# Down-projection weight sums taken by DRAM transfers during gate and up, paced by that stage

## The chip, the cores and the metric

One core of a Trainium2 chip runs the whole program. The metric is device time in microseconds (us), the median of several executions; lower is better. PE is TensorE (matrix products), DVE is VectorE, ACT is ScalarE, POOL is GpSimd and SP is SyncE, which here only issues DMA transfers. The kernel is written with a scheduling layer that decides the order on every engine when the program is built and adds all semaphore waits; on the chip every engine runs its list strictly in order.

## The reference, cut to what matters

The reference is one step of a two-layer backbone. In every layer a token mixer is followed by this channel mixer, on 640 tokens (512 + 128) of width 1024, with 2816 hidden units:

```python
def swiglu(h, w_gate_up, w_down):
    g, u = jnp.split(h @ w_gate_up, 2, axis=-1)
    return (jax.nn.silu(g) * u) @ w_down

    h2 = rmsnorm(x, g_pre_ffn) * (1.0 + scale2) + shift2
    x = x + gate2 * rmsnorm(swiglu(h2, w_gate_up, w_down), g_post_ffn)
```

All data are float32. The kernel splits each factor into a high and a low part (`split`, lines 211 and 217: ACT writes the rounded high part, DVE the difference) and takes three products per block (`mm3`, lines 227 to 229).

## The kernel before, in words

**Gate and up** (`gate_up`) makes the hidden activations in 22 steps of 128 units, j = 0 to 21; j = 0 and 1 are plain, the other twenty (`fast`) use seven products in place of eight (Strassen's scheme). Each step loads two blocks of 512 KB of weights by SP (line 969; I call them the first and the second load of a step) into `raw`, a pool of three buffers. `prep` makes four sums of quarters of these blocks on DVE (line 214, tile `sw`) and splits seven operands into `w` tiles, one step ahead of PE. The first sum (`sw<-raw,raw`) needs both loads. PE adds several products into one PSUM bank that ACT and DVE read in between, so PE waits if those reads are late; the last such read is DVE's `s<-ps,s` ahead of the seventh product. The result is `hid` (line 951). In layer 0 a list of background steps (`self.bg`) stands beside it: 8 loads of 1 MB and 32 DVE steps (tile `acc`) for the modulation of layer 1, one for each 6.6 us of the program's own count of time (`clk`).

**The down projection** (`w_down`) is Strassen's scheme over the whole stage: the hidden units are split in two (e), the output columns in two (h), and seven phases run one after another, in this order: p1, p2, p5, p6, p3, p7, p4. Each goes over six groups of hidden units, g = 0 to 5, a group holding 512 KB of weights per (e, h), the last one 256 KB. Phases p1, p2, p3 and p7 take 99 matrix instructions, p5, p6 and p4 take 66. Per group the phase splits the weights into `w` (`wsplit`) and the activations into `hs` (`xsplit`). p1, p2 and p3 use the blocks as they are. The other phases use sums of them:

- p5 uses W(0,0) + W(0,1), p6 adds W(1,1) to that, p4 adds W(1,0) as well. The running sum lies in SBUF in three `wk` tiles (`V`, filled by p1's load, line 1076); after each split POOL adds the next block by a DMA that accumulates (`add`, line 1079).
- p7 uses W(0,1) + W(1,1): SP loads the first into `raw` (`fresh`, line 1083), POOL adds the second by an accumulating DMA into the same buffer, and then ACT and DVE split it (line 1239).

So the POOL queue carries 24 accumulating DMAs per layer in the down projection. The normalisations (`rsq`, lines 248 to 252) are on the same queue. From p7 on, `begin` (line 1156), `finish` and `end` bring in the residual of finished tokens by SP, finish them on ACT, POOL and DVE (line 917) and store them by SP (line 1170); in layer 0 they are also prepared for the next layer. The `hs` tiles and these `work` tiles come from one pool of 12 buffers (`Q`).

Of the kernel before, what the change touches and what calls it, by code (L numbers as in the profile page):

```python
# [10 lines left out]
F32 = mybir.dt.float32  # L11
R = mybir.dt.float32r
AF = mybir.ActivationFunctionType
ALU = mybir.AluOpType
# [117 lines left out]
class Trunk:  # L132
# [811 lines left out]
    def gate_up(self, l, pre):  # L944
        nc, a, blk = self.nc, self.a, self.blk
        hid = [self.Q([4, N], F32, "hid") for i in range(NJ // 4)]

# [38 lines left out]
        def fast(j, ops, nxt):  # L986
# [13 lines left out]
            u, v = self.S(), self.S()  # L1000
# [20 lines left out]
            product(C, a12, blk[1][0], True, g11)  # L1021
            product(A, a22, t4, False, lambda: out(j, 0, A, g0, nc.vector))

        ws = [[self.load(a["w_gu"][l, j, u]) for u in range(2)] for j in range(NPLAIN)]
# [9 lines left out]
        for j in range(NPLAIN):  # L1034
            plain(j, ws[j], 1)
            for _ in range(8):
                next(nxt, None)
# [6 lines left out]

    def w_down(self, l, src, hid, gg, nxt):

# [11 lines left out]
        dd = [self.Q([3, 2, 384], F32, "dd") for _ in range(2)]  # L1058
        V = [None] * 3

# [8 lines left out]

        def vg(g):  # L1070
            return V[g // 2][:, (g % 2) * 1024 : (g % 2) * 1024 + cnt(g) * 512]

        def into(g, e, h):
            if V[g // 2] is None:
                V[g // 2] = self.W()
            nc.sync.dma_start(out=vg(g), in_=dram(e, h, g))

        def add(dst, e, h, g):
            nc.gpsimd.dma_start(out=dst, in_=dram(e, h, g), accum_op=ALU.add)

        def fresh(g, e, h):
            r = self.raw()[:, 0 : cnt(g) * 512]
            nc.sync.dma_start(out=r, in_=dram(e, h, g))
            return r

        def wsplit(g, s):
# [89 lines left out]
        def p1(g):  # L1176
            into(g, 0, 0)
            w = wsplit(g, vg(g))
            add(vg(g), 0, 1, g)
# [9 lines left out]
        def p2(g):  # L1189
            w = wsplit(g, fresh(g, 1, 0))  # L1190
            return xsplit(g, [x(g, 1)[:, :, A4]]), w
# [13 lines left out]
        def p5(g):  # L1205
            w = wsplit(g, vg(g))
            add(vg(g), 1, 1, g)
            return xsplit(g, [d(g)[:, :, 128:384]]), w
# [5 lines left out]
        def p6(g):  # L1214
            w = wsplit(g, vg(g))
            add(vg(g), 1, 0, g)
            s = d(g)[:, :, 128:384]
# [8 lines left out]
        def p3(g):  # L1226
            w = wsplit(g, fresh(g, 1, 1))
            s = d(g)[:, :, 128:384]
# [8 lines left out]
        def p7(g):  # L1237
            r = fresh(g, 0, 1)
            add(r, 1, 1, g)
            w = wsplit(g, r)  # L1240
            h = self.Q([2, 2, 384], R, "hs")
# [7 lines left out]
        def p4(g):  # L1249
            return xsplit(g, [x(g, 1)[:, :, B4]]), wsplit(g, vg(g))  # L1250

# [90 lines left out]
    def run(self):  # L1342
# [4 lines left out]
        for l in range(L):  # L1347
# [20 lines left out]
            pre = self.w_down(l, x, hid, gg, nxt)  # L1368
            if l + 1 < L:
# [41 lines left out]
```

## Time and profile before

| | us |
|---|---|
| median of 3 runs (lowest, highest) | 1390.4 (1387.85, 1395.24) |
| time of the profiled execution | 1396.39 |
| span of its trace, first to last instruction | 1394.5 |
| gate and up from j = 2 to the end, layer 0 | 318.4 to 568.4 |
| down projection, layer 0 | 568.4 to 716.6 |
| gate and up from j = 2 to the end, layer 1 | 996.1 to 1242.9 |
| down projection, layer 1 | 1242.9 to 1387.2 |
| tail after the last matrix instruction | 1387.2 to 1394.5 |

Read it as a line with two places of interest in each layer: the stage of gate and up, some 250 us, and the down projection behind it, some 145 us. The borders are the starts of the first matrix instruction of each stage. A matrix instruction is shown as busy for longer than the distance to the next one, because they are pipelined; so phases with the same number of instructions are compared by their length and not by their busy time.

### The profile page before, as it was taken

Reading aid. Unit: us, or ns where it says so; the run is one execution under the profiler, and the core shown is the slowest. Engines: PE = TensorE matmul, PEld = TensorE weight load, DVE = VectorE, ACT = ScalarE, POOL = GpSimd, SP = SyncE. Lnnn points to the kernel's source line nnn. Section 1 sums busy time; section 2 is a strip of 40 time slices with the busy share of each in tenths; the row PEclk is TensorE's granted clock in tenths of the full one; section 3 lists DMA queues with packets and bytes.
Section 4 is the critical chain, followed back from the end, with each engine's and each line's share of the span. In section 5 each row is a group of like instructions: output and inputs, shape, how many; then the busy total and the mean of one; then the engine's idle time right before and its main releaser. Section 6 shows DMA issues by size and latency. Waiting matters only on the chain.

```text
span 1394.5 us, 21421 instructions
## 1 busy us (share of the span) xinstructions
PE 1342.1 (96%) x8188; PEld 1206.2 (86%) x8188; DVE 1023.3 (73%) x1794; ACT 692.0 (50%) x1398; POOL 151.3 (11%) x186
## 2 busy tenths in 40 slices
PE   5899999999999999999899999999999999999996
PEld 2788977899999999888688998878999999998875
DVE  3789476499988985776788956757977777675955
ACT  4543275465554554545583324746644544444633
POOL 1101121110000000111211101302000000010220
PEclk9999999999999999999999999999999999999998
DMA  9555247244333333768655533553222322375982
GB/s 373 168 166 184 82 147 241 99 146 143 125 108 106 120 121 110 194 139 192 183 181 184 186 112 121 176 204 124 73 92 91 90 78 85 98 184 126 183 211 97
DMA packets 57974, 203.68 MB, mean 146 GB/s; under 512 B 7488, under 2 KB 8384, under 8 KB 56848
## 3 DMA queue, kind: packets, MB, share of 16 engines
q1 hardware_dynamic: 50960, 179.25, 38.7%
q0 software_dynamic: 6912, 23.07, 9.4%
q8 instruction: 64, 1.05, 0.3%
q14 instruction: 38, 0.31, 0.1%
HBM read 191.61 MB, written 10.68 MB: 145 GB/s over the span
## 4 chain that ended last, share of the span: by engine, by line
PE 71%; DMA 9%; DVE 8%; issue 5%; ACT 4%; POOL 2%; POOLq 0%; DVEq 0%; SPq 0%; ACTq 0%
PE ps L227 22%; PE ps L229 22%; PE ps L228 22%; DMA raw<-in_w_dn 4%; PE ps L240 2%; DVE w L217 2%; DVE acc L377 2%; PE ps L284 2%; ACT w L211 2%; DMA raw<-in_w_out 1%; PE ps L829 1%; POOL rt L252 1%; DMA raw<-in_ada 1%; DMA raw<-in_w_vpc 1%; DMA raw<-in_w_b 1%
## 5 line engine op out<-in xcount | busy, mean ns | idle before, releaser
L217 DVE TENSOR_TENSOR w<-raw,w 128x512 fp32r<-128x512 f32 (+2 forms) x220 | 197.5, 903 | 105.5 <-ACT w L211 104.0
L211 ACT ACTIVATE w<-raw 128x512 fp32r<-128x512 f32 (+2 forms) x220 | 175.4, 801 | 185.5 <-PE ps L229 74.8
L227 PE MATMUL ps<-T,w 128*128 128x320 f32 x640 | 198.5, 310 | 0.0
L229 PE MATMUL ps<-T,w 128*128 128x320 f32 x640 | 197.8, 309 | 0.0
L228 PE MATMUL ps<-T,w 128*128 128x320 f32 x640 | 197.7, 309 | 0.0
L227 PE MATMUL ps<-b,w 128*128 128x320 f32 x608 | 188.1, 309 | 0.0
L228 PE MATMUL ps<-b,w 128*128 128x320 f32 x608 | 187.9, 309 | 0.0
L229 PE MATMUL ps<-b,w 128*128 128x320 f32 x608 | 187.9, 309 | 0.0
L227 PE MATMUL ps<-w,hs 128*128 128x512 f32 x396 | 156.7, 396 | 6.6 <-ACT cc L211 4.6
L229 PE MATMUL ps<-w,hs 128*128 128x512 f32 x396 | 156.4, 395 | 5.5 <-DVE hs L217 5.4
L228 PE MATMUL ps<-w,hs 128*128 128x512 f32 x396 | 156.3, 395 | 0.2 <-DVE w L217 0.2
L211 ACT ACTIVATE w<-sw 128x512 fp32r<-128x512 f32 x160 | 96.3, 625 | 77.3 <-PE ps L229 65.3
L211 ACT ACTIVATE s<-ps 128x320 f32<-128x320 f32 (+2 forms) x148 | 65.3, 443 | 129.1 <-PE ps L229 105.9
L214 DVE TENSOR_TENSOR s<-ps,s 128x320 f32<-128x320 f32 (+1 forms) x144 | 68.7, 482 | 80.1 <-PE ps L229 79.9
L227 PEld LDWEIGHTS ps<-T,w 128*128 128x128 f32 x640 | 120.1, 188 | 2.1 <-issue 1.7
L228 PEld LDWEIGHTS ps<-T,w 128*128 128x128 f32 x640 | 120.1, 188 | 0.0
L229 PEld LDWEIGHTS ps<-T,w 128*128 128x128 f32 x640 | 120.1, 188 | 0.0
L227 PEld LDWEIGHTS ps<-b,w 128*128 128x128 f32 x608 | 114.1, 188 | 0.4 <-ACT s L211 0.3
L228 PEld LDWEIGHTS ps<-b,w 128*128 128x128 f32 x608 | 114.1, 188 | 0.1
L229 PEld LDWEIGHTS ps<-b,w 128*128 128x128 f32 x608 | 114.1, 188 | 0.0
L217 DVE TENSOR_TENSOR w<-sw,w 128x512 fp32r<-128x512 f32 x160 | 106.2, 686 | 5.1 <-ACT w L211 3.1
L227 PEld LDWEIGHTS ps<-w,hs 128*128 128x128 f32 x396 | 75.6, 191 | 23.8 <-ACT cc L211 5.4
(236 smaller groups left out, 2856.3 us busy)
## 6 DMA issues: line engine op xcount, KB each, us to landing
raw<-in_w_gu SPq DMA_DIRECT2D x88, 512.0 KB, 3.5
raw<-in_ada SPq DMA_DIRECT2D x64, 512.0 KB, 4.3
raw<-in_w_dn SPq DMA_DIRECT2D x30, 512.0 KB, 4.3
wk<-in_w_dn POOLq DMA_DIRECT2D x30, 512.0 KB, 6.2
ada<-in_ada SPq DMA_DIRECT2D x8, 1024.0 KB, 15.5
raw<-in_w_out SPq DMA_DIRECT2D x16, 512.0 KB, 4.1
wk<-in_ada SPq DMA_DIRECT2D x8, 1024.0 KB
xs<-work SPq DMA_DIRECT2D x15, 512.0 KB, 4.6
```

Source lines behind the costliest of these rows:

```text
L211: self.nc.scalar.activation(out, in_, f, **kw)
L214: self.nc.vector.tensor_tensor(out, x, y, op=op)
L217: self.nc.vector.tensor_tensor(lo, src, hi.bitcast(F32), op=ALU.subtract)
L227: mm(out, lh, rh, start=start, stop=False, skip_group_check=more)
L228: mm(out, lh, rl, start=False, stop=False, skip_group_check=more)
L229: mm(out, ll, rh, start=False, stop=stop, skip_group_check=more)
L240: self.nc.tensor.transpose(out, in_, self.ident)
L252: self.nc.gpsimd.tensor_tensor(r2, r, self.mhalf[:, :n], op=ALU.pow)
L284: self.nc.tensor.matmul(ps[32 * j : 32 * j + 32, :], self.cond[:, k, :], s, start=start, stop=stop, tile_position=(0, 32 * j))
L377: nc.vector.scalar_tensor_tensor(acc[:, s], raw, c, acc[:, s], op0=ALU.mult, op1=ALU.add)
L829: self.nc.tensor.matmul(ps[64 * e : 64 * e + 64, :], lhs[e], rhs[e], start=start, stop=stop, tile_position=(0, 64 * e))
```

## The change

The sums are made in DRAM during gate and up instead of in SBUF during the down projection. A new function `queue_sums` makes a list of 36 steps for POOL. They fill four scratch arrays in DRAM, v0 to v3, each with six groups: v0 = W(0,0) + W(0,1), v2 = W(0,1) + W(1,1), v1 = v0 + W(1,1), v3 = v1 + W(1,0). A sum is a copy from DRAM to DRAM and an accumulating DMA with its target in DRAM; the first 12 steps hold two DMAs each (v0 and v2), the other 24 one each, which makes 48 per layer. Each step begins with a copy of one element of `hid` by POOL, so that its transfers wait until gate and up has written that element. The steps go into the background list, in layer 0 alternating with those that were there; the distance of the list becomes 215 us divided by its length, and it starts later. In the down projection every phase now loads by SP into `raw` and splits from there: p5 from v0, p6 from v1, p7 from v2, p4 from v3.

```diff
+            self.pace = hid[j // 4][:, j % 4, 0:1]      # end of fast(j); plain(j) sets it too
...
+    def queue_sums(self, l):
+        v = [[self.dp.tile([128, 1040], F32, ...)[:, 0 : (2 if g < 5 else 1) * 512] for g in range(6)] for i in range(4)]
+        def copy(i, g, s):
+            nc.gpsimd.dma_start(out=v[i][g], in_=s)
+        def add(i, e, h, g):
+            nc.gpsimd.dma_start(out=v[i][g], in_=dram(e, h, g), accum_op=ALU.add)
+        def paced(f):
+            def go():
+                t = self.M([1], "pace", 2)
+                ins = nc.gpsimd.tensor_copy(t, self.pace)
+                with self.tc.issue_after(ins.ins):
+                    f()
+            return go
...
         def p7(g):
-            r = fresh(g, 0, 1)
-            add(r, 1, 1, g)
-            w = wsplit(g, r)
+            w = wsplit(g, vs[2][g])
...
         def p4(g):
-            return xsplit(g, [x(g, 1)[:, :, B4]]), wsplit(g, vg(g))
+            return xsplit(g, [x(g, 1)[:, :, B4]]), wsplit(g, vs[3][g])
...
+            vs, qs = self.queue_sums(l)
             if l + 1 < L:
                 mod1, q = self.queue_ada_w(l + 1, 0)
-                self.bg, self.bg_last = [(6.6, f) for f in q], self.now + 12.0
+                qs = [x for k in range(max(len(q), len(qs))) for x in (*q[k : k + 1], *qs[k : k + 1])]
+            self.bg, self.bg_last = [(215.0 / len(qs), f) for f in qs], self.now + 30.0
```

How the lists of the engines change, in layer 1. First POOL around gate and up, before the change: behind the last normalisation (`rs`, `rt`) of the stage ahead there stand at once the accumulating DMAs of the down projection into `wk`.

```order
L250 TENSOR_SCALAR rs_9536<-ms_9534 128x1
L252 TENSOR_TENSOR rt_9538<-rs_9536,mhalf 128x1
L1079 DMA wk_12374<-in_w_dn 128x1024 x2
L1079 DMA wk_12411<-in_w_dn 128x1024 x2
L1079 DMA wk_12466<-in_w_dn 128x1024
L1079 DMA wk_12466<-in_w_dt 128x512
```

The same place after it (`v` is a scratch array in DRAM, `pace` the copied element):

```order
L250 TENSOR_SCALAR rs_9719<-ms_9717 128x1
L252 TENSOR_TENSOR rt_9721<-rs_9719,mhalf 128x1
L1067 COPY pace_10135<-hid_9687 128x1
L1058 DMA v_9663<-in_w_dn 128x1024
L1058 DMA v_9675<-in_w_dn 128x1024
L1067 COPY pace_10211<-hid_9687 128x1
L1058 DMA v_9664<-in_w_dn 128x1024
L1058 DMA v_9676<-in_w_dn 128x1024
```

The waits on `hid` and the transfers now stand between the two stages' normalisations, where POOL had nothing in this stage. Next POOL at p7 of layer 1 before the change, with the additions into `raw` ahead of the normalisation of the first finished tokens:

```order
L1079 DMA raw_13115<-in_w_dn 128x1024
L1079 DMA raw_13151<-in_w_dn 128x1024
L1079 DMA raw_13187<-in_w_dn 128x1024
L248 TENSOR_SCALAR rs_13218<-mso_12363 128x1
L252 TENSOR_TENSOR rt_13220<-rs_13218,mhalf 128x1
L1079 DMA raw_13232<-in_w_dt 128x512
L248 TENSOR_SCALAR rs_13225<-mso_12364 128x1
```

After it, the last paced sums are directly followed by those normalisations:

```order
L1067 COPY pace_12567<-wk_12425 128x1
L1061 DMA v_9685<-in_w_dn 128x1024
L1067 COPY pace_12620<-wk_12425 128x1
L1061 DMA v_9686<-in_w_dt 128x512
L248 TENSOR_SCALAR rs_13525<-mso_12666 128x1
L252 TENSOR_TENSOR rt_13527<-rs_13525,mhalf 128x1
L248 TENSOR_SCALAR rs_13532<-mso_12667 128x1
```

The additions have left this place. Last, SP from the end of p7's loads on, layer 1, before the change (`work<-xs` is the load of a residual, `out_y_s<-work` the store of finished tokens):

```order
L1083 DMA raw_13187<-in_w_dn 128x1024
L278 DMA work_13146<-xs_9019 128x1024
L1083 DMA raw_13232<-in_w_dt 128x512
L278 DMA work_13182<-xs_9019 128x1024
L1170 DMA out_y_s<-work_13146 128x1024
L1170 DMA out_y_s<-work_13182 128x1024
```

After it, where v_9679 and v_9680 belong to p7 and v_9681 to v_9686 to p4:

```order
L1110 DMA raw_13495<-v_9679 128x1024
L1110 DMA raw_13539<-v_9680 128x512
L1110 DMA raw_13554<-v_9681 128x1024
L1110 DMA raw_13591<-v_9682 128x1024
L278 DMA work_13455<-xs_9178 128x1024
L1110 DMA raw_13611<-v_9683 128x1024
L1194 DMA out_y_s<-work_13455 128x1024
L278 DMA work_13490<-xs_9178 128x1024
L1110 DMA raw_13642<-v_9684 128x1024
L1110 DMA raw_13667<-v_9685 128x1024
L1194 DMA out_y_s<-work_13490 128x1024
L1110 DMA raw_13692<-v_9686 128x512
```

The six loads of p4, which were not there before, now stand among the loads and stores of the finished tokens. In layer 1 the lists of PE, ACT and DVE are otherwise the same up to the last step of gate and up; in layer 0 the background steps stand at other places in DVE's list.

## Rows read from the trace of the kernel before

**Rows 1.** The page: busy time of PE, its share of the span, and instructions.

```profile
PE 1342.1 (96%) x8188; PEld 1206.2 (86%) x8188; DVE 1023.3 (73%) x1794; ACT 692.0 (50%) x1398; POOL 151.3 (11%) x186
```

**Rows 2.** Busy time by stretch. Each row: from and to, length, then busy us and instructions of PE, PEld, DVE, ACT and POOL, the granted TensorE clock, the DMA share and GB/s. In order: gate and up of layer 0 and of layer 1; layer 0's p5 with p6, p3, p7, p4; layer 1's p3, p7, p4.

```profile
318.40:568.40 250.00, 250.00 (x1705) 247.50 (x1705) 215.99 (x357) 125.72 (x244) 2.83 (x3) 1.00 0.39 122
996.10:1242.90 246.80, 246.75 (x1683) 246.47 (x1682) 179.85 (x316) 122.30 (x239) 1.82 (x2) 1.00 0.32 99
...
613.30:643.20 29.90, 29.90 (x133) 24.76 (x132) 27.51 (x38) 19.57 (x31) 8.77 (x10) 1.00 0.99 181
643.20:665.70 22.50, 22.50 (x101) 18.60 (x101) 12.60 (x17) 11.16 (x17) 2.65 (x3) 1.00 0.74 174
665.70:697.70 32.00, 26.40 (x100) 20.11 (x99) 22.21 (x34) 16.11 (x30) 7.25 (x11) 0.89 0.68 190
697.70:716.60 18.90, 18.19 (x93) 15.03 (x92) 17.35 (x34) 16.09 (x36) 3.05 (x6) 1.00 0.55 182
...
1317.70:1340.20 22.50, 22.50 (x101) 18.62 (x100) 14.66 (x20) 11.59 (x18) 2.60 (x3) 1.00 0.80 197
1340.20:1367.50 27.30, 23.04 (x101) 18.32 (x99) 16.95 (x25) 12.40 (x22) 5.20 (x7) 1.00 0.67 193
1367.50:1387.20 19.70, 17.94 (x66) 13.97 (x66) 10.50 (x16) 6.86 (x14) 2.21 (x4) 0.83 0.18 63
```

**Rows 3.** PE's waits by releaser in the down projection, first layer 0 (568.4 to 716.6), then layer 1 (from 1242.9): us in total, times, the longest.

```profile
PE ps L229 <- DVE hs L217: 4.0, 2, 2.7
PE ps L227 <- ACT hs L211: 2.0, 2, 1.3
...
PE ps L227 <- ACT cc L211: 4.6, 2, 2.8
PE ps L229 <- DVE hs L217: 1.4, 1, 1.4
```

**Rows 4.** The timeline in p7, two rows of ACT and one of DVE of layer 0, one of ACT of layer 1: start, length, engine, line, operation, tile; in brackets the idle time of the engine ahead of it and what ended it.

```profile
661.71 1.06 ACT L211 ACTIVATE w<-raw 128x1024 fp32r<-128x1024 f32 x1 [7.30 <-DMA raw<-in_w_dn]
...
677.76 1.06 ACT L211 ACTIVATE w<-raw 128x1024 fp32r<-128x1024 f32 x1 [8.37 <-DMA raw<-in_w_dn]
...
678.85 1.23 DVE L217 TENSOR_TENSOR w<-raw,w 128x1024 fp32r<-128x1024 f32 x1 [7.61 <-ACT w L211]
...
1349.59 1.06 ACT L211 ACTIVATE w<-raw 128x1024 fp32r<-128x1024 f32 x1 [4.77 <-DMA raw<-in_w_dn]
```

**Rows 5.** The timeline of PE at the end of p7, two rows of layer 0 and two of layer 1.

```profile
687.86 0.50 PE L229 MATMUL ps<-w,hs 128*128 128x512 f32 x1 [2.75 <-DVE hs L217]
...
691.37 0.63 PE L227 MATMUL ps<-w,hs 128*128 128x512 f32 x1
...
1367.46 0.50 PE L227 MATMUL ps<-w,hs 128*128 128x512 f32 x1 [2.84 <-ACT cc L211]
...
1370.16 0.80 PE L227 MATMUL ps<-w,hs 128*128 128x512 f32 x1 [1.74 <-ACT cc L211]
```

**Rows 6.** The page: DMA queues with packets, MB and their share of 16 engines' span (q1 is SP's, q0 POOL's), and DMA issues with KB each and the median us to landing.

```profile
q1 hardware_dynamic: 50960, 179.25, 38.7%
q0 software_dynamic: 6912, 23.07, 9.4%
...
raw<-in_w_gu SPq DMA_DIRECT2D x88, 512.0 KB, 3.5
...
raw<-in_w_dn POOLq DMA_DIRECT2D x10, 512.0 KB, 7.8
```

**Rows 7.** Time from issue to landing (least, median, most): SP's loads into `raw` in gate and up of layer 1 (1020 to 1230); a load into `raw` beside POOL's additions (1312 to 1320); POOL's additions in p5 (1279 to 1300).

```profile
DMA to landing us min/median/max: 3.4/3.5/3.5
...
DMA to landing us min/median/max: 6.1/6.1/6.1
...
DMA to landing us min/median/max: 5.3/5.5/6.8
```

**Rows 8.** The timeline of one step of gate and up in layer 1: the issue of a second load by SP; four rows of DVE, the last one the first sum that needs that load; the first matrix instruction of the seventh product.

```profile
1162.08 0.33 SPq L969 DMA_DIRECT2D raw<-in_w_gu  x1
...
1161.36 0.69 DVE L217 TENSOR_TENSOR w<-raw,w 128x512 fp32r<-128x512 f32 x1 [1.89 <-ACT w L211]
...
1163.96 0.49 DVE L214 TENSOR_TENSOR s<-ps,s 128x320 f32<-128x320 f32 x1 [1.31 <-PE ps L229]
...
1165.77 0.48 DVE L214 TENSOR_TENSOR s<-ps,s 128x320 f32<-128x320 f32 x1
1166.17 0.68 DVE L214 TENSOR_TENSOR sw<-raw,raw 128x512 f32<-128x512 f32 x1
...
1167.21 0.31 PE L227 MATMUL ps<-T,w 128*128 128x320 f32 x1
```

**Rows 9.** Gate and up of layer 0: busy time in four stretches of two steps each (columns as in rows 2), and DVE's waits for weights there.

```profile
367.60:392.30 24.70, 24.70 (x171) 24.70 (x170) 23.55 (x38) 12.32 (x25) 0.00 (x0) 1.00 0.38 128
392.30:416.90 24.60, 24.60 (x169) 24.48 (x168) 18.77 (x34) 11.81 (x25) 0.00 (x0) 1.00 0.39 130
...
441.50:468.00 26.50, 26.50 (x184) 26.49 (x183) 26.22 (x45) 14.10 (x28) 0.00 (x0) 1.00 0.37 120
468.00:492.60 24.60, 24.60 (x170) 24.60 (x169) 23.38 (x38) 12.05 (x24) 0.00 (x0) 1.00 0.38 112
...
DVE sw L214 <- DMA raw<-in_w_gu: 4.6, 6, 1.5
```

More of the change, by code (lines that the diff above doesn't have):

```diff
@@ L945, in gate_up @@
         nc, a, blk = self.nc, self.a, self.blk
+        self.pace = None
         hid = [self.Q([4, N], F32, "hid") for i in range(NJ // 4)]
@@ L1035, in gate_up @@
             plain(j, ws[j], 1)
+            self.pace = hid[0][:, j, 639:640]
             for _ in range(8):
@@ L1043, in gate_up, with dram, w_down @@
         return hid
-    def w_down(self, l, src, hid, gg, nxt):
+    def queue_sums(self, l):
+        nc, a = self.nc, self.a
+        v = [[self.dp.tile([128, 1040], F32, tag=f"v{i}{g}", name=self.nm("v"))[:, 0 : (2 if g < 5 else 1) * 512] for g in range(6)] for i in range(4)]
+        def dram(e, h, g):
+            return a["w_dn"][l, e, h, g] if g < 5 else a["w_dt"][l, e, h]
+        def copy(i, g, s):
[9 more added lines that the diff above has]
+            return go
+        todo = []
+        for g in range(6):
+            todo.append(lambda g=g: [copy(0, g, dram(0, 0, g)), copy(2, g, dram(0, 1, g))])
+        for g in range(6):
+            todo.append(lambda g=g: [add(0, 0, 1, g), add(2, 1, 1, g)])
+        for i, (e, h) in ((1, (1, 1)), (3, (1, 0))):
+            for g in range(6):
+                todo.append(lambda g=g, i=i: copy(i, g, v[0 if i == 1 else 1][g]))
+            for g in range(6):
+                todo.append(lambda g=g, i=i, e=e, h=h: add(i, e, h, g))
+        return v, [paced(f) for f in todo]
+    def w_down(self, l, src, hid, gg, vs, nxt):
         a, nc = self.a, self.nc
@@ L1058, in w_down @@
         dd = [self.Q([3, 2, 384], F32, "dd") for _ in range(2)]
-        V = [None] * 3
         def x(g, e):
@@ L1068, in dram, with wsplit @@
             return a["w_dn"][l, e, h, g] if g < 5 else a["w_dt"][l, e, h]
[L1070 to L1086, printed above, removed]
+        def wsplit(g, src):
+            s = self.raw()[:, 0 : cnt(g) * 512]
+            nc.sync.dma_start(out=s, in_=src)
             w = self.wp.tile([128, 2, 1024], R, tag="w", name=self.nm("w"))
@@ L1176, in p1 @@
         def p1(g):
-            into(g, 0, 0)
-            w = wsplit(g, vg(g))
-            add(vg(g), 0, 1, g)
+            w = wsplit(g, dram(0, 0, g))
             h = xsplit(g, [x(g, 0)[:, :, A4]])
@@ L1189, in p2 @@
         def p2(g):
-            w = wsplit(g, fresh(g, 1, 0))
+            w = wsplit(g, dram(1, 0, g))
             return xsplit(g, [x(g, 1)[:, :, A4]]), w
@@ L1205, in p5 @@
         def p5(g):
-            w = wsplit(g, vg(g))
-            add(vg(g), 1, 1, g)
+            w = wsplit(g, vs[0][g])
             return xsplit(g, [d(g)[:, :, 128:384]]), w
@@ L1214, in p6 @@
         def p6(g):
-            w = wsplit(g, vg(g))
-            add(vg(g), 1, 0, g)
+            w = wsplit(g, vs[1][g])
             s = d(g)[:, :, 128:384]
@@ L1226, in p3 @@
         def p3(g):
-            w = wsplit(g, fresh(g, 1, 1))
+            w = wsplit(g, dram(1, 1, g))
             s = d(g)[:, :, 128:384]
@@ L1367, in run @@
                 nxt = (mod1, h, src)
-            pre = self.w_down(l, x, hid, gg, nxt)
+            pre = self.w_down(l, x, hid, gg, vs, nxt)
             if l + 1 < L:
```

## The prediction

> **What bounds the kernel now.** I read four views in this order. The page first: PE is busy for 96% of the span [rows 1], so the whole idle time of PE is some 52 us, and a change that leaves PE's work as it is can win back only part of that. Then the busy time by stretch: gate and up has no gap on PE at all, 250.00 of 250.00 us in layer 0 and 246.75 of 246.80 in layer 1 [rows 2]. In the down projection p3 takes 22.5 us in both layers and p5 with p6 29.9, at full clock and without a gap, but p7, with the same 99 matrix instructions as p3, takes 32.0 and 27.3 us, and p4, with the 66 of p5 or p6 (14.95 us each), takes 18.9 and 19.7 [rows 2]. So the room is in p7 and p4. Third, PE's waits: there PE waits on DVE and ACT for operands, 4.0 us in layer 0, 4.6 in layer 1 in the largest rows [rows 3]. Fourth, what those engines waited for: in p7 ACT sat idle for 7.30, 8.37 and 4.77 us until a weight block had landed, and DVE 7.61 us behind ACT [rows 4]. Those are the blocks that POOL adds into: an addition into `raw` lands 7.8 us (median) after its issue, against 3.5 for a plain load of gate and up [rows 6], and in p7 it stands between SP's load and the split, with only three `raw` buffers. ACT and DVE work in order, so the finishing of tokens behind them came late as well, and the `hs` tiles behind that: the gaps of 2.75, 2.84 and 1.74 us at the end of p7 [rows 5]. After them the granted clock fell: its mean is 0.89 in layer 0's p7 and 0.83 in layer 1's p4, 1.00 elsewhere [rows 2], and a matrix instruction is shown with 0.63 us in that time, against 0.50 or less [rows 5]; that is the lower level, 1.2 GHz in place of 2.4.
>
> **What the change removes.** All 24 additions per layer leave the down projection. By length, p7 and p4 stand above their gapless like by 32.0 − 22.5 = 9.5 us and 0.7 us (the gap of PE in 18.90 us; the rest of that stretch is other PE work) in layer 0, and by 27.3 − 22.5 = 4.8 and 19.7 − 14.95 = 4.75 us in layer 1 [rows 2]. Sum **19.75 us**. Of that the lower clock makes (1 − 0.89) × 32.0 = 3.5 and (1 − 0.83) × 19.7 = 3.3 us, which go only if the gaps ahead of it go. Behind a plain load, p7 needs per group 3.5 us of load, 1.06 of ACT and 1.23 of DVE [rows 4, 7], 5.8 us on three buffers, 1.9 us per group, against 22.5 / 6 = 3.75 us of PE. So the load no longer limits p7. What is late next is the finishing of tokens, whose operations stand in DVE's list between the last `hs` tiles of p7, and the reuse of `Q` buffers behind it; I leave for it the largest gap of each layer as it is, 2.75 and 2.84 us [rows 5], without a fall of the clock. Gain: 19.75 − 5.6 = 14.1, taken as **14 us**; bounds 7 (the clock still falls in both layers, 14 − 6.8) and 19.75. POOL's normalisations no longer stand behind additions; that is part of the same gain.
>
> **What it adds in the down projection.** SP's loads go from 24 to 42 per layer, all through `raw`. In p5 and p6 a group takes 14.95 / 6 = 2.49 us of PE, against the 1.9 us above, so the loads keep up, with 3 × 2.49 − 5.8 = 1.7 us per round for queueing on ACT and DVE (DVE is busy for 27.51 of 29.9 us there, as before [rows 2]). If a load took the 6.1 us that one took beside additions [rows 7], a group would take 8.4 / 3 = 2.8 us, 0.3 × 12 = 3.7 us per layer. I take 0, because the additions that made 6.1 of 3.5 are gone and the DMA share of 0.99 [rows 2] falls with them; if that cover is missing it costs up to 7.4. In p4 the loads stand in SP's list behind the stores of finished tokens, which wait for DVE's line 917: the last load waits for two postnorms. p4 reaches its last group only after p7's 22.5 us, and I count nothing.
>
> **What it adds in gate and up.** Per layer 24 additions move in and 24 copies are new. Their price in DMA time: POOL's queue before moved 23.07 MB, all additions, in 9.4% of 1394.5 = 131 us of all 16 engines, 0.303 us per packet; SP's 179.25 MB in 540 us, 0.169 per packet [rows 6]. A layer's additions take 65.5 us. A copy from DRAM to DRAM, and an addition whose target is in DRAM, is nowhere in this trace. For copies the bounds are SP's rate and POOL's: 35 or 65 us; for additions I take POOL's rate, the nearest row, and let them be half again as dear at the upper end. So 100 to 165 us of engine time are spread over 250, on a share of 0.39 and 0.32 [rows 2]: it fits, but what runs beside it is slowed.
>
> What is slowed is the second load of each step. In layer 1 it is issued at 1162.08, lands 3.5 us later, and the first DVE sum that needs it starts at 1166.17: 0.6 us of room [rows 7, 8]. A load has 8 packets per engine; behind one addition packet each it takes 8 × 0.303 = 2.4 us more, behind copy packets 1.4. The row beside additions says the same: 6.1 − 3.5 = 2.6 [rows 7]. Behind that sum DVE's list holds the reads of PSUM that PE needs; each must be done before the seventh product (1165.77 + 0.48, used at 1167.21: 0.96 us to spare). In layer 1 DVE idles 1.89 and 1.31 us per step [rows 8], so 0.6 + 1.89 swallow 2.4 to 2.6 whole: **0 us**, at most 1 per step. In layer 0 DVE carries the background steps too. Where it idles by 5.8 us in two steps a late load costs nothing, but in stretches with 1.15, 0.3 and 1.2 us idle it does [rows 9]. About 5.5 steps with additions fall there, each between 0 and 2.4 − 0.5 = 1.9 us. In the trace DVE waited for these loads 6 times in 20 steps [rows 9], so in most it was later than the load; I take 0.7 × 5.5 = **4 us**, bounds 0 and 10.5.
>
> The paced waits themselves cost nothing: behind a waiting POOL there are only more of these steps, and the next that anybody waits for are the normalisations of p7, some 100 us on. v0 and v2 come first in the list and are done in its first third, v3 is needed last. POOL's issue takes no time of another engine.
>
> A rule speaks to this place. The Trainium skill, "DMA: Bandwidth & Descriptors", section "Anatomy of one DMA — SWDGE (gpsimd) path", fits a POOL transfer at about 2.0 us plus bytes over 436 GB/s, 3.2 us for 512 KB. The trace does not agree: 5.5 us for an addition [rows 7]. By the rule an addition's packets would be as short as a copy's, layer 0's 4 us would be some 1, and the sum would end 3 us lower.
>
> **Sum.** −14 + 4 = −10 us. The profiled execution took 1396.4 us (span 1394.5), so 1386; the median of the runs shown is 6 us under it, and the same 10 us give **1380**.
>
> **The rivals.** *Paid back.* The second loads gate DVE in all saturated steps of layer 0 (10.5 us): 14 − 10.5 = 3.5 us are left, 1387. For it: landing and first use are 0.6 us apart in layer 1 [rows 8]. Against: the 6 waits in 20.
>
> *The waits stay in p7.* The finishing of tokens, with SP's list now interleaving p4's loads and stores, still holds up the last `hs` tiles, and the clock falls again: the gain is 7, less 4 is 3 us, 1387. For it: the waits of PE name `hs` and `cc`, not the block [rows 3]. Against: DVE and ACT had stood idle for those 7 to 8 us just ahead [rows 4], which is what made their lists late.
>
> *Slower.* An accumulating packet whose target is in DRAM has to read and write there. If it occupies an engine for twice the 0.303 us, a second load comes 4.8 us late: in layer 1 1.3 us beyond what the step swallows (0.6 + 1.89 + 0.96) in some 10 steps with additions, 13 us; in layer 0 4.3 × 5.5 + 2.0 × 4.5 = 33 us; less 14 it is 32 us slower, 1422. At half again the packet (3.6 us late) layer 0 pays 3.1 × 5.5 + 0.8 × 4.5 = 21 us and the time is 1397. It decides from about 1.3 times the packet of before, where layer 0 alone pays 14. For it: no row shows such a packet, and PE has no gap to hide anything in gate and up. Against: the engines had room. The Trainium skill, same page, section "Queues, rings and completion order", says that an engine takes turns between queues packet by packet; by that a long packet of POOL's delays each packet of SP's, and the 6.1 beside 3.5 agrees [rows 7].
>
> *The change doesn't do what it says*, with sums not ready when p5 wants them: against it speak the 100 to 165 us of engine time that the list needs in 250, and that v0 is at its head; 1390 to 1400.
>
> **How the numbers follow.** A measurement of this kernel can tell about 0.5%, 7 us, from no change. Forecast 1380 (1371 to 1383): 0.55. Paid back, 1387: 0.16. Waits stay, 1387: 0.11. Slower, 1397 to 1422: 0.15. Not as said: 0.03. Faster by over 0.5%: the forecast and a little of the paid-back case, 0.57. Slower: 0.15 and half of the last, 0.16. Same: 0.27. The range leaves out the full gain without any cost (1390.4 − 19.75 = 1371 is its lower end) and most of the slower case: 1371 to 1394.
>
> **What would show it.** Right: p7 near 23 us in both layers, no ACT wait on `raw<-in_w_dn` there, clock 1.00 in p7 and p4, POOL's queue at 46 MB, HBM written up by 46 MB, gate and up of layer 0 longer by about 4 us and of layer 1 by less than 1. Wrong: PE waits in gate and up on DVE sums of more than 10 us in total, a POOL packet well above 0.30 us, or p7 still above 27 us with waits on `hs`.

## The result: slower by 1.5%, and the profile after

The changed kernel takes **1410.7 us** (median of 4 runs, 1406.4 to 1413.4) against 1389.1 us for the kernel before on the same chip: a ratio of 1.0147, 95% interval 1.0103 to 1.0191. The profiled execution took 1410.8 us, with a span of 1409.0.

First the page of the changed kernel, the lines that answer to [rows 1, 6]: PE's busy time; the two queues with packets, MB and share; and POOL's issues into the scratch arrays, with KB each and the median us to landing.

```profile
PE 1346.1 (96%) x8188; PEld 1210.4 (86%) x8188; DVE 1026.1 (73%) x1794; ACT 692.3 (49%) x1398; POOL 231.5 (16%) x306
...
q1 hardware_dynamic: 56144, 196.55, 41.8%
q0 software_dynamic: 13312, 46.14, 13.4%
...
v<-in_w_dn POOLq DMA_DIRECT2D x60, 512.0 KB, 7.4
...
v<-v POOLq DMA_DIRECT2D x20, 512.0 KB, 5.2
```

Then its busy time by stretch, columns as in [rows 2]: gate and up of layer 0 and of layer 1; layer 0's p5 with p6, p7, p4; layer 1's p7, p4; then four stretches of a step or so: two of layer 0 with the longest stalls, and two of layer 1, one without a stall and the longest.

```profile
317.90:588.00 270.10, 255.17 (x1705) 251.26 (x1705) 218.35 (x359) 125.58 (x242) 58.46 (x84) 0.98 0.69 198
1004.50:1267.10 262.60, 251.65 (x1683) 249.49 (x1682) 181.25 (x320) 122.41 (x242) 63.65 (x84) 0.99 0.61 174
632.90:662.90 30.00, 30.00 (x134) 24.82 (x134) 27.85 (x38) 19.98 (x31) 0.00 (x0) 1.00 0.58 178
...
685.30:707.80 22.50, 22.50 (x101) 18.62 (x100) 17.64 (x28) 14.15 (x26) 4.79 (x8) 1.00 0.61 208
707.80:726.10 18.30, 18.21 (x93) 14.94 (x92) 16.60 (x35) 15.10 (x35) 3.20 (x6) 1.00 0.69 220
...
1364.40:1386.80 22.40, 22.40 (x101) 18.54 (x100) 18.24 (x27) 13.28 (x25) 4.36 (x4) 1.00 0.65 228
1386.80:1401.90 15.10, 15.10 (x67) 12.20 (x65) 4.55 (x8) 2.58 (x8) 1.73 (x4) 1.00 0.16 63
...
354.80:372.70 17.90, 13.71 (x86) 13.45 (x85) 12.79 (x20) 6.47 (x13) 3.30 (x6) 0.93 0.65 215
385.50:406.20 20.70, 14.02 (x85) 13.76 (x85) 11.25 (x18) 4.72 (x9) 2.70 (x3) 0.87 0.71 183
...
1055.70:1068.00 12.30, 12.30 (x86) 12.30 (x86) 6.23 (x11) 5.66 (x11) 4.11 (x6) 1.00 0.83 197
...
1097.10:1114.20 17.10, 14.09 (x86) 13.82 (x86) 9.99 (x19) 5.79 (x12) 2.65 (x5) 0.90 0.61 178
```

The reader is to see two things that pull apart. In the down projection the gaps are gone: p7 is 22.5 and 22.4 us without a gap (32.0 and 27.3 before), layer 1's p4 15.1 (19.7), and the clock is 1.00 there. By the borders of the stages layer 0's down projection went from 148.1 to 138.0 us and layer 1's from 144.3 to 134.8: **19.6 us won**. But gate and up, where PE had no gap, is 270.1 us long in place of 250.0 and 262.6 in place of 246.8 by these stretches; by the first matrix instruction of each stage **20.1 and 15.9 us lost**. 36.0 − 19.6 = 16.4; the other stages came out 1.9 us shorter, which makes the 14.5 us between the two spans.

The medians lie 21.6 us apart, not 14.5, because the profiled execution of the kernel before was 7 us above its median and that of the changed kernel at its own. So the 19.6 us are the gain against one execution. In the trace of run 5 below, whose down projection is that of the kernel before, it took 147.5 and 140.6 us, 15.3 more than in the changed kernel; in that of run 8 17.3 more. The row of run 5's layer 1 (144.3 above):

```profile
1240.30:1380.90 140.60, 136.70 (x596) 112.12 (x594) 98.54 (x131) 69.90 (x110) 25.34 (x30) 0.99 0.69 161
```

By the medians 36.0 − 21.6 = 14.4 us are won outside gate and up. The gain is some 14 to 20 us.

What PE and DVE waited for in gate and up of the changed kernel, by releaser (us in total, times, longest), first layer 0, then layer 1:

```profile
PE ps L227 <- DVE s L214: 14.9, 7, 6.7
...
DVE sw L214 <- DMA raw<-in_w_gu: 17.4, 11, 3.4
...
DVE acc L410 <- DMA wk<-in_ada: 9.9, 4, 5.8
...
PE ps L227 <- ACT s L211: 11.0, 8, 3.0
...
DVE sw L214 <- DMA raw<-in_w_gu: 24.1, 11, 5.9
DVE sw L214 <- issue: 14.9, 4, 4.8
```

`sw<-raw,raw` is the sum that needs a step's second load; before, DVE waited for it 4.6 us in layer 0 [rows 9]. (The row with "issue" is the same sum; the landing it waited for is not in the trace.) The wait for `wk<-in_ada` is another one: a 1 MB load of layer 0's background steps. The timeline shows how both reach PE. Layer 0, rows of SP, DVE and PE: the load is issued at 389.18 and its first `acc` step begins at 401.13, 12 us later; behind that in DVE's list stands the read of PSUM that PE needs.

```profile
389.18 0.38 SPq L395 DMA_DIRECT2D wk<-in_ada  x1
...
401.13 1.29 DVE L410 SCALAR_TENSOR_TENSOR acc<-wk,cond,acc 128x1024 f32<-128x1024 f32 x1 [5.76 <-DMA wk<-in_ada]
402.33 0.48 DVE L214 TENSOR_TENSOR s<-ps,s 128x320 f32<-128x320 f32 x1
...
402.87 0.64 PE L227 MATMUL ps<-T,w 128*128 128x320 f32 x1 [6.68 <-DVE s L214]
```

Layer 1, rows of DVE, ACT and PE: the late sum holds DVE's reads, these ACT's activation, and that PE's seventh product.

```profile
1100.27 0.69 DVE L214 TENSOR_TENSOR sw<-raw,raw 128x512 f32<-128x512 f32 x1 [5.92 <-DMA raw<-in_w_gu]
...
1102.39 0.47 ACT L211 ACTIVATE s<-s 128x320 f32<-128x320 f32 x1 [5.74 <-DVE s L214]
...
1103.76 0.41 PE L227 MATMUL ps<-T,w 128*128 128x320 f32 x1 [3.01 <-ACT s L211]
```

After the long gaps the granted clock falls too: 0.87 over the 20.7 us from 385.5 is some (1 − 0.87) × 20.7 = 2.7 us of that stretch.

### The profile page after: what moved, and what is told of

Same layout as the page of the kernel before. It is cut to its first block, busy times and chain, and to the rows that moved or that the text cites. A ratio compares the mean times of both kernels' runs of the same rounds, so it can differ in the third digit from the quotient of the medians.

```text
span 1409.0 us, 21612 instructions
## 1 busy us (share of the span) xinstructions
PE 1346.1 (96%) x8188; PEld 1210.4 (86%) x8188; DVE 1026.1 (73%) x1794; ACT 692.3 (49%) x1398; POOL 231.5 (16%) x306
## 4 chain that ended last, share of the span: by engine, by line
PE 61%; DVE 13%; DMA 12%; issue 8%; ACT 3%; POOL 2%; DVEq 0%; POOLq 0%; ACTq 0%; SPq 0%
PE ps L227 19%; PE ps L228 18%; PE ps L229 18%; DMA raw<-in_w_gu 5%; DVE w L217 3%; DVE acc L377 2%; DMA raw<-in_ada 2%; PE ps L240 2%; DMA wk<-in_ada 2%; PE ps L284 2%; DVE sw L214 2%; DMA raw<-in_w_out 1%; DVE s L214 1%; ACT w L211 1%; POOL rt L252 1%
## 5 line engine op out<-in xcount | busy, mean ns | idle before, releaser
L211 ACT ACTIVATE w<-raw 128x1024 fp32r<-128x1024 f32 (+2 forms) x268 | 221.5, 831 | 129.2 <-PE ps L229 47.0
L217 DVE TENSOR_TENSOR w<-raw,w 128x1024 fp32r<-128x1024 f32 (+2 forms) x268 | 252.7, 947 | 40.4 <-ACT w L211 39.4
L227 PE MATMUL ps<-T,w 128*128 128x320 f32 x640 | 201.3, 315 | 25.5 <-DVE s L214 14.9
L229 PE MATMUL ps<-T,w 128*128 128x320 f32 x640 | 199.9, 312 | 0.0
L228 PE MATMUL ps<-T,w 128*128 128x320 f32 x640 | 199.6, 312 | 0.0
L227 PE MATMUL ps<-w,hs 128*128 128x512 f32 x396 | 154.4, 390 | 0.1
L228 PE MATMUL ps<-w,hs 128*128 128x512 f32 x396 | 154.1, 389 | 0.0
L229 PE MATMUL ps<-w,hs 128*128 128x512 f32 x396 | 153.9, 389 | 0.0
L227 PEld LDWEIGHTS ps<-T,w 128*128 128x128 f32 x640 | 121.5, 190 | 30.6 <-DVE s L214 16.8
L1067 POOL COPY pace<-hid 128x1 f32<-128x1 f32 x66 | 60.7, 920 | 396.5 <-DVE hid L952 396.5
L228 PEld LDWEIGHTS ps<-T,w 128*128 128x128 f32 x640 | 121.8, 190 | 0.0
L229 PEld LDWEIGHTS ps<-T,w 128*128 128x128 f32 x640 | 121.7, 190 | 0.0
L227 PEld LDWEIGHTS ps<-b,w 128*128 128x128 f32 x608 | 115.6, 190 | 1.0 <-ACT s L211 0.9
L228 PEld LDWEIGHTS ps<-b,w 128*128 128x128 f32 x608 | 115.3, 190 | 0.1
L229 PEld LDWEIGHTS ps<-b,w 128*128 128x128 f32 x608 | 115.1, 189 | 0.0
```

The lines of the kernel that those rows point to most:

```text
L211: self.nc.scalar.activation(out, in_, f, **kw)
L217: self.nc.vector.tensor_tensor(lo, src, hi.bitcast(F32), op=ALU.subtract)
L227: mm(out, lh, rh, start=start, stop=False, skip_group_check=more)
L228: mm(out, lh, rl, start=False, stop=False, skip_group_check=more)
L229: mm(out, ll, rh, start=False, stop=stop, skip_group_check=more)
L1067: ins = nc.gpsimd.tensor_copy(t, self.pace)
```

## The experiments

Times are medians, ratios are to the kernel before on the same chip; "stage" is gate and up from the first matrix instruction of j = 2 to that of p1, in the profiled execution (before: 250.1 us in layer 0, 246.7 in layer 1). Runs 5 and 8 were executed once each (1389.9 and 1401.6 us) and are read by the steps in their traces, not by their time.

**1. The list without its transfers** (`no_transfers`).

```diff
         def copy(i, g, s):
-            nc.gpsimd.dma_start(out=v[i][g], in_=s)
+            pass
...                                  # add() likewise
+        v = [[dram(e, h, g) for g in range(6)] for e, h in ((0, 1), (1, 1), (0, 1), (1, 0))]
```

> The changed kernel with its 48 transfers per layer left out; the paced one-element copies and the order of every list stay, and the down projection loads plain blocks of w_down in place of v0 to v3, so the sums are missing from its result. Theory Shared queues (the stalls of gate and up come from the transfers that run beside the weight loads): all 35 us of stalls in gate and up go and the 19.6 us won in the down projection stay, 1368 to 1373 us, ratio to before near 0.986. Rival List (the stalls come from the new order of the background list and from the paced copies, so that DVE stands at an acc step whose 1 MB load is late): the 20 us in layer 0 stay, about 1390, ratio near 1.00.

Measured 1375.0 us, 0.9903 (0.9868 to 0.9938). The stages:

```profile
313.30:566.50 253.20, 250.97 (x1706) 247.57 (x1705) 219.16 (x359) 126.22 (x244) 23.03 (x36) 1.00 0.38 124
983.50:1230.60 247.10, 246.93 (x1682) 246.40 (x1682) 181.62 (x319) 124.06 (x242) 27.73 (x36) 1.00 0.27 91
```

Layer 1's stall is gone (247.1), layer 0 keeps 3.1 us of its 20. So the transfers make 33 of the 36 us; the new order of layer 0's background steps makes 3, and the paced copies nothing in layer 1. The time is 2 us above the expected range; those 3 us would account for it.

**2. Additions made plain copies** (`add_as_copy`): `accum_op=ALU.add` left out of `add`.

> The changed kernel with each of the 24 additions per layer made a plain copy into the same scratch array, so v0 to v3 hold single blocks and the sums are missing. A 4 KB packet of an addition took 0.328 us (median), one of a copy 0.159. If the stalls go with the engine time that the transfers take from the loads, half of the additions' part falls away: stalls of 35 us become 15 to 20, 1390 to 1396 us. If each transfer costs the loads a fixed delay whatever its packets last (a late first packet), the stalls stay above 28 us: 1403 to 1411.

Measured 1394.0 us, 1.003 (1.0006 to 1.0054). Stages 263.0 and 256.3 us: 13 and 9.5 us lost in place of 20 and 16. The time is in the first range, but the 22.5 us of stalls are above the 15 to 20 that it was made from. The cost goes down with the engine time that the packets take; the number of transfers alone does not set it.

**3. The transfers started in the middle of a step** (`mid_step`).

```diff
             def u12():
                 self.tt(c22, A, c22, ALU.add)
                 out(j, 1, c22, g1, nc.vector)
+                self.pace = hid[j // 4][:, j % 4, 320:321]
...
-            self.pace = hid[j // 4][:, j % 4, 0:1]
```

> The changed kernel with one edit: the paced copies wait for the other half of hid, which a step writes some 4 us earlier, after the second weight load of the step has been used and some 4 us before the next first load is issued; all 48 transfers and sums stay. Theory Phase (the transfers hurt since they start together with the two weight loads of a step): the 35 us of stalls fall to 10 or less, 1370 to 1382 us. Rival Room (the queues are too full in this stage wherever the transfers stand): 1403 or more.

Measured 1423.4 us, 1.025 (1.0208 to 1.0292): the theory Phase fell. The stages are 278.6 and 264.9 us. A burst that starts there stands ahead of both loads of the next step and not only of the second; the longest wait of the sum is 7.2 us in place of 5.9. And the last bursts of the stage now stand ahead of the first blocks of the down projection: 5.0 us of PE's wait at the end of layer 1 are new. The two rows are DVE's in layer 1's stage and PE's at its end:

```profile
DVE sw L214 <- DMA raw<-in_w_gu: 31.8, 14, 7.2
...
PE ps L227 <- ACT s L211: 5.0, 1, 5.0
```

**4. Only p7's sum in DRAM, one transfer at a time** (`v2_end`, and again as `v2_again`). The rest is the kernel before.

```diff
+        todo = []
+        for g in range(6):
+            todo.append(lambda g=g: nc.gpsimd.dma_start(out=v[g], in_=dram(0, 1, g)))
+            todo.append(lambda g=g: nc.gpsimd.dma_start(out=v[g], in_=dram(1, 1, g), accum_op=ALU.add))
...
         def p7(g):
-            r = fresh(g, 0, 1)
-            add(r, 1, 1, g)
+            r = self.raw()[:, 0 : cnt(g) * 512]
+            nc.sync.dma_start(out=r, in_=vs[g])
...
+                for k, f in enumerate(q):            # layer 0; in layer 1 one every 16.0
+                    self.bg.append((6.6, f))
+                    if k % 3 == 2 and qs:
+                        self.bg.append((0.0, qs.pop(0)))
```

> The kernel before with only p7's sum made in DRAM during gate and up: 12 paced transfers per layer, one at a time, at the pace point of the change; the other sums stay additions into SBUF in the down projection, and layer 0's background steps keep their distance of 6.6. All sums are made. Theory Shared queues: most of the 19.6 us in p7 and p4 is won, and with one transfer per step instead of two to four the stalls of gate and up are 0 to 10 us: 1371 to 1381. If each transfer costs what it costs in the change (35 us for 96, 0.36 us each), 24 cost 9 us: about 1380. If the fixed price of a paced step is what hurts, however few they are: 1390 or more.

> The kernel with only p7's sum made in DRAM, one transfer at a time, again with more rounds: 1368 to 1375 us, ratio to before 0.985 to 0.991.

Measured 1372.1 us, 0.9887 (0.985 to 0.9925), and again 1375.6 us, 0.9904 (0.9887 to 0.9921): **faster than both kernels**. The stages and both layers' p7 and p4:

```profile
317.60:567.70 250.10, 250.10 (x1707) 247.62 (x1706) 216.37 (x352) 125.87 (x244) 19.12 (x26) 1.00 0.47 142
980.90:1228.10 247.20, 246.63 (x1682) 246.37 (x1681) 179.32 (x315) 122.04 (x239) 18.93 (x26) 1.00 0.41 122
664.90:687.40 22.50, 22.50 (x101) 18.61 (x100) 18.38 (x29) 14.39 (x27) 5.68 (x8) 1.00 0.45 150
687.40:706.20 18.80, 18.09 (x93) 14.94 (x92) 17.79 (x35) 15.99 (x36) 3.13 (x6) 1.00 0.52 179
1325.40:1347.80 22.40, 22.40 (x100) 18.58 (x99) 18.55 (x28) 13.65 (x26) 3.97 (x4) 1.00 0.46 168
1347.80:1363.00 15.20, 15.16 (x67) 12.20 (x65) 7.50 (x12) 4.26 (x10) 2.19 (x4) 1.00 0.11 44
```

Gate and up has its old length, with 12 transfers per layer beside it, and the down projection nearly all of the change's gain (138.5 and 134.8 us). So the additions of p5, p6 and p4 had cost nothing in the down projection; p7's alone had. By the medians 16.7 and 13.1 us are won. The first expectation held and the second set came out 0.6 us above its range; the price of 0.36 us per transfer did not hold.

**5. Bursts of known size** (`ladder`), into the kernel before, with two quiet steps behind each.

```diff
+            if l == 1 and j in LADDER:              # {4: (4, 0), 7: (1, 1), 10: (2, 1), 13: (3, 1), 16: (4, 1), 19: (2, 0)}
+                t = self.M([1], "pace", 2)
+                ins = nc.gpsimd.tensor_copy(t, hid[(j - 1) // 4][:, (j - 1) % 4, 0:1])
+                with self.tc.issue_after(ins.ins):
+                    n, kw = LADDER[j]
+                    for g in range(n):
+                        nc.gpsimd.dma_start(out=v[g], in_=a["w_dn"][l, kw, 0, g], **({"accum_op": ALU.add} if kw else {}))
```

> The kernel before with extra transfers of POOL in layer 1's gate and up alone, into scratch arrays that nobody reads (extra work, nothing left out), each burst issued at the pace point of the change and followed by two quiet steps: in step 4 four copies, step 7 one addition, step 10 two additions, step 13 three, step 16 four, step 19 two copies, 512 KB each. A step of layer 1 lasts 12.32 us without a stall and can take a second load that is 3.45 us late (0.6 + 1.89 + 0.96). Theory Burst (the two loads of a step are 16 packets per engine in one queue, and while POOL has packets waiting each of them lets one of POOL's 0.328 us or 0.159 us go first): one addition makes the second load 2.6 us late, stall 0; two 5.2, stall 1.8; three and four 1.8, or 3.8 if the first packet of a load also comes 2 us late; four copies 2.5 or 4.5 late, stall 0 to 1.1; two copies 0. Rival Work (each transfer costs the same, 35 us over 96 of them): 0.36 us per transfer, so 0.4, 0.7, 1.1, 1.5 for one to four additions. Rival Start (any transfer that is ahead of a load delays it by the same): one addition costs as much as four.

By the starts of PE's steps one and two additions and two copies cost 0, three additions 0.9, four 1.1, four copies 0.3 us, each in the step behind. DVE's timeline has the sum that waited after two, three and four additions (after one there is no wait):

```profile
1101.98 0.69 DVE L217 TENSOR_TENSOR sw<-raw,raw 128x512 f32<-128x512 f32 x1 [1.97 <-DMA raw<-in_w_gu]
...
1140.53 0.69 DVE L217 TENSOR_TENSOR sw<-raw,raw 128x512 f32<-128x512 f32 x1 [3.56 <-DMA raw<-in_w_gu]
...
1178.63 0.69 DVE L217 TENSOR_TENSOR sw<-raw,raw 128x512 f32<-128x512 f32 x1 [3.78 <-DMA raw<-in_w_gu]
```

With the 0.6 us of room [rows 7, 8], the load was 2.6, 4.2 and 4.4 us late; after one addition it landed 3.8 us after its issue in place of 3.4. Rivals Work and Start fall; Burst overrated every burst of additions.

The packet records of the trace show where the lateness comes from. In a quiet step the second load's first packet starts 1.0 us after the issue, and its packets then take 2.1 to 2.4 us. After two, three and four additions its first packet starts 3.4 to 3.5 us after the issue, and its packets then take 2.2, 3.4 and 3.7 us. So the 2.6 us after two additions are nearly all a late first packet; why it is late stays open. The prediction had put down 2.4 us for eight packets behind one addition packet each: about the right number, by luck. The Trainium skill, "DMA: Bandwidth & Descriptors", section "Queues, rings and completion order", lets an engine take turns between queues packet by packet; the longer stretches of 3.4 and 3.7 us, in which both queues had packets, agree with it, but it does not cover the late first packet. And four additions were not quite a burst of four: POOL issued the last one some 5 us behind the third.

**6. The same 12 transfers per layer in bursts** (`v2_burst`): two lists of four and of two in place of single ones, 8 background steps or 48.0 apart.

> The kernel with only p7's sum made in DRAM (12 transfers per layer), with one edit: the same transfers are issued in bursts of four copies, four additions, two copies, two additions in place of one at a time; the pace point, the sums and the bytes are the same. Theory Burst: the single transfers cost nothing, the bursts cost 1 (four copies) + 4 (four additions) + 0 + 2 (two additions) = 7 us in layer 1 and as much or more in layer 0: 14 to 20 us above the single form, 1386 to 1392. Rival Work: as the single form, 1370 to 1376.

Measured 1380.3 us, 0.9935 (0.9912 to 0.9958), 8 us above the single form of run 4 (5 above its second set). Stages 256.5 and 249.5 us, 6.4 and 2.3 us longer than in the single form; the largest stall, 4.0 us, follows layer 0's first burst. Same bytes, same sums: the burst itself costs, less than expected, and the rival Work falls.

**7. All 48 transfers, as single paced steps** (`single`), and these at two points of a step (`both_points`, with the added line of run 3 and the old one kept).

```diff
-            todo.append(lambda g=g: [copy(0, g, dram(0, 0, g)), copy(2, g, dram(0, 1, g))])
+            todo.append(lambda g=g: copy(0, g, dram(0, 0, g)))
+            todo.append(lambda g=g: copy(2, g, dram(0, 1, g)))
...                                  # the additions of v0 and v2 likewise
```

> The changed kernel with the 12 paced steps of two transfers taken apart into 24 of one, 48 paced steps in the same 215 us: about two transfers per step of gate and up everywhere, where the change has four in the first third and one or two later. All sums stay. Theory Burst: steps with four transfers held 25 of the 35 us of stalls; with two copies a step costs 0, with two additions up to 1.8: 5 to 20 us of stalls in all, 1377 to 1394. Rival Work (the number of transfers decides): 35 us stay, 1403 to 1412.

> The kernel with 48 single paced steps, with one edit: the paced copy waits for whichever half of hid was written last in program order, so the transfers of a step start at two points of it, some 4 us apart, in place of together at its end. Theory Burst: one transfer at a time costs nothing, so this is 0 to 10 us below the form with one point: 1370 to 1385. Rival Phase (what starts in the middle of a step stands ahead of the next loads and hurts more, as in the form with all transfers in the middle, 1423): 5 to 15 us above the form with one point.

Measured 1391.1 us, 0.9997 (0.9973 to 1.0021), and 1397.0 us, 1.0062 (1.0035 to 1.0089). With two transfers per step in place of four, 20 us of the loss come back with the same work; the rival Work falls here too. The second form is the slower one, as Phase had it; in its profile some 7 of 13 us in layer 1 fall in the last step of the stage, for the reason given in run 3. The stages of `single`:

```profile
315.20:568.80 253.60, 251.10 (x1706) 247.57 (x1705) 217.23 (x359) 124.58 (x242) 65.14 (x92) 1.00 0.71 206
984.80:1241.00 256.20, 250.19 (x1683) 248.00 (x1682) 181.60 (x320) 121.72 (x240) 73.25 (x90) 0.99 0.61 173
```

The DMA share is as high as in the changed kernel (0.71 and 0.61), and layer 0 loses 3.5 us, not 20: the share does not tell the cost. (This profiled execution is 6 us below the median of its runs.)

**8. Bursts in steps that follow one another** (`ladder2`): the table of run 5 made `{3: (4, 0), 5..9: (2, 1), 12..14: (4, 1), 17..19: (4, 0)}`.

> The kernel before with extra transfers of POOL in layer 1's gate and up alone, into scratch arrays that nobody reads, as in the first run of bursts, but now in steps that follow one another: four copies in step 3; two additions in each of steps 5 to 9; four additions in each of 12 to 14; four copies in each of 17 to 19. Alone, two additions had cost PE 0, four 1.1 us and four copies 0.3 us. Theory Carry (a late step starts its loads late and close together, so the next burst meets a step with no room left; four additions are 4 x 8 x 0.328 = 10.5 us of engine time, with the loads over 12.32): the five steps of two additions cost 3 to 8 us in all, the three of four additions 7 to 10 as in the change (2.0, 2.5, 4.8), the three of four copies 1 to 4. Rival No carry (each burst costs what it costs alone): 0, 3.3 and 0.9 us.

The five steps with two additions cost 1.5 and 3.6 = 5.1 us, where one alone costs 0; the three with four additions 1.0 and 2.4 = 3.4 us, the last three bursts of copies 0.7. The four copies in step 3, which stand alone, cost 1.5 in the step behind, where they cost 0.3 in run 5: a lone burst varies by over 1 us. The 5.1 us are what Carry expected. For four additions the cost is that of bursts alone, but the row was not the one that was meant: POOL issued its third burst at 1155.83, behind the second load of that step (1155.27) and not ahead of it. Two rows show the carry: a step with two additions inside the row that costs nothing, and the last one, where the lateness comes out (length 15.90 against 12.32, clock 0.89); and DVE's wait in each.

```profile
1068.40:1080.70 12.30, 12.30 (x85) 12.30 (x85) 9.02 (x17) 5.91 (x12) 4.53 (x3) 1.00 0.52 133
1093.00:1108.90 15.90, 14.12 (x86) 13.86 (x85) 11.57 (x22) 6.15 (x13) 0.00 (x0) 0.89 0.29 86
...
1080.45 0.69 DVE L217 TENSOR_TENSOR sw<-raw,raw 128x512 f32<-128x512 f32 x1 [2.47 <-DMA raw<-in_w_gu]
...
1094.99 0.69 DVE L217 TENSOR_TENSOR sw<-raw,raw 128x512 f32<-128x512 f32 x1 [4.69 <-DMA raw<-in_w_gu]
```

In a quiet step of layer 1 that sum starts 2.8 us before PE's step; here it came 1.9 and 0.1 us before, 0.3 before, and at last 2.0 us after it. The loads, which a quiet step issues 1.6 and 5.4 us after its start, went out at 4.1 and 5.9 in the last of these steps, together with the next additions: a late step begins with less room than a quiet one.

**9. The old distance for layer 0's background steps** (`keep_lead`): distance 6.6 for them and 0 for the paced steps between, in place of one even distance.

> The changed kernel with one edit in layer 0's list: the background steps of the modulation keep the distance of 6.6 that they had before, and the paced sums stand between them; so their loads of 1 MB are issued some 15 us ahead of their first use again, where the change left 9 to 12. All sums and the double transfers of the first 12 paced steps stay, layer 1 is as in the change. Theory Lead (about half of layer 0's 20 us are acc steps that wait for a 1 MB load and stand in DVE's list ahead of the reads of PSUM; 9.9 us of such waits): layer 0 stalls 6 to 12 us, 1396 to 1404. Rival (the second weight loads alone would have stalled the same steps): 17 us or more, 1406 to 1412.

Measured 1406.8 us, 1.0132 (1.0106 to 1.0158); layer 0's stage 274.0 us. The time is in the rival's range, but the run is inconclusive on its question: the lead did not come back (issue to first use 10.4 and 9 us at the first two stalls, in place of some 15), and the waits at `acc` grew to 14.5 us.

**10. Without seven of the eight 1 MB loads** (`one_ada_load`).

```diff
         def fetch():
             if order:
                 half, kk = order.pop(0)
+                if "one" in box:
+                    raws.append(box["one"])
+                    return
-                raw = self.W()
+                raw = box["one"] = self.W()
```

> The changed kernel with one edit in layer 0's background list: of its eight loads of 1 MB for the modulation of layer 1 only the first is made and all its steps read that block, so seven loads and the right modulation of layer 1 are left out; the DVE steps, all 48 transfers, and layer 1 stay. In the change DVE waited 9.9 us for these loads at acc steps and layer 0's gate and up was 20 us longer. Theory Third load (the 1 MB loads, which stand behind the bursts like the weight loads and whose acc steps stand in DVE's list ahead of the reads of PSUM, make more than half of that): layer 0's stage 4 to 9 us longer than before, 1395 to 1400. Rival (the second weight loads stall the same steps without them): 14 us or more longer, 1404 to 1412.

Measured 1389.2 us, 1.001 (0.9987 to 1.0032). Layer 0's stage (the row ends 0.06 us behind it):

```profile
314.70:570.00 255.30, 250.80 (x1706) 247.60 (x1705) 218.64 (x360) 125.71 (x242) 58.24 (x84) 1.00 0.66 181
...
DVE sw L214 <- DMA raw<-in_w_gu: 15.6, 12, 3.6
```

5.2 us longer than before in place of 20.1, with every transfer of the change beside it: Third load held. The second row is DVE's wait for the weight loads in that stage, 15.6 us against 17.4 in the changed kernel; so those loads were about as late as before, and what is gone is the wait at `acc`. The time fell below its range; layer 1 lost only 8.7 us in this profile. (The profiled execution is 5 us below the median.)

## Why the prediction was wrong

1. **The gain**, 14: about right. Against the one profile that the forecast was worked out from it is 19.6 us, near the upper bound of 19.75, and neither the 5.6 us left for "what is late next" nor the lower clock stayed. But that execution was a long one; other traces of the same down projection put the gain at 15.3 and 17.3 us, the medians of run 4 at 13.1 and 16.7, those of the change at 14.4. So the loss is not a matter of this term.
2. **Loads of the down projection, 0**: right. p5 with p6 takes 30.0 us (29.9 before).
3. **The price of a packet**: right. In the packet records a 4 KB packet of an addition took 0.328 us (median) in the kernel before, with its target in SBUF, and 0.328 in run 5's bursts, in DRAM; a copy's took 0.159. (The 0.303 is a mean that holds shorter packets too.) So the rival *Slower* named the place and the sign, and its range (1397 to 1422) holds the time, but its mechanism, a longer packet when the target is in DRAM, is not what happened.
4. **Layer 1, 0 us: wrong by 15.9.** This step failed: "0.6 + 1.89 swallow 2.4 to 2.6 whole". A quiet step with two additions did swallow 2.6 us (run 5). But the sum took every step for a quiet one, with one packet of POOL ahead of each of the second load's. The change issues two to four transfers in one step, in steps that follow one another; four additions occupy an engine for 4 × 8 × 0.303 = 9.7 us of a step of 12.32. Then the second load's first packet is late as well as its packets slowed (4.2 to 4.4 us in run 5), and a late step issues its own loads late, so that the next burst meets less room. The changed kernel's trace shows this carry in the three steps with four additions and in the one behind: SP's issue of the second load, 5.4, 8.0, 8.5 and 9.3 us after the starts of steps 6 to 9, where a quiet step has 5.4.

```profile
1061.10 0.33 SPq L970 DMA_DIRECT2D raw<-in_w_gu  x1
...
1075.99 0.33 SPq L970 DMA_DIRECT2D raw<-in_w_gu  x1
...
1090.80 0.33 SPq L970 DMA_DIRECT2D raw<-in_w_gu  x1
...
1106.39 0.33 SPq L970 DMA_DIRECT2D raw<-in_w_gu  x1
```

   Steps 7, 8 and 9 came out 2.0, 2.5 and 4.8 us longer. Taking the bursts apart (run 7) or having few (run 4) gives the time back.
5. **Layer 0, 4 us: wrong by 16.** The term for the second loads was of the right size, partly by luck: without the 1 MB loads the stage loses 5.2 us (run 10), but half of it in one step (2.7), where the sum had 0.7 in each of 5.5. This step failed too by what it put at nothing. What was left out is a third load: the sum priced the background steps only as DVE work. Their 1 MB loads meet the same bursts, and their `acc` steps stand in DVE's list ahead of the reads of PSUM. The two longest gaps of PE there, 4.2 and 6.7 us, stand right behind such steps, and without those loads 15 us of the 20 are gone (run 10).
6. **"It fits", 100 to 165 us of engine time in 250**: true of the mean (share 0.69 and 0.61) and of no use. A step of layer 1 at a share of 0.83 lost nothing, one at 0.61 4.8 us: PE stalls where late loads meet bursts.
7. **The paced waits, 0**: right for layer 1 (run 1); the new order of layer 0's list cost 3 us that the sum did not have.

What stays open is the size of layer 1's loss. The list of layer 1 is the same in the changed kernel and in runs 9 and 10, and their profiles show 15.9, 11.2 and 8.7 us. Run 8's three steps of four additions cost 3.4 us against 9.3 in the changed kernel's steps 7 to 9; that only two of its bursts stood ahead of the loads would go that way, but it isn't shown to be the whole difference. What makes the first packet of a load late is open as well.

## What to carry to other kernels

A transfer that is moved into a stage without gaps is to be priced against the next transfer that somebody waits for, in the fullest step and with what the step before leaves over, not against the mean share of the queues. List every load that meets it there, those of background steps too, and what stands behind the waiting instruction in its engine's list. Move only the part that had a price where it was (here one sum of four), one transfer at a time.

## What the runs showed of the hardware

A 4 KB packet of an addition by DMA into DRAM took as long as one into SBUF, 0.328 us (point 3). Two additions of 512 KB issued together with a load made the load behind it 2.6 us late, three 4.2 and four 4.4: most of it is a first packet that starts 3.4 to 3.5 us after the issue in place of 1.0, whatever the number (run 5). A DMA share of 0.71 stood beside a loss of 3.5 us in one kernel and 0.69 beside 20.1 in another (run 7, layer 0).
